# Moving three block loads from GpSimd's queue to SyncE's, and a new place for the quarters in the load order

## The chip, the cores and the metric

The kernel runs on one NeuronCore of a Trainium2 chip. The core has five engines with a queue of instructions each: TensorE (PE: matmuls, and transposes through a matmul), VectorE (DVE), ScalarE (ACT), GpSimd (POOL) and SyncE (SP, which here only issues DMAs). They wait for each other by semaphores. Sixteen DMA engines move data between HBM and SBUF; SP, ACT and POOL each feed them through a queue of their own. The metric is the device time of one execution in microseconds, the median of several runs; lower is better.

## The reference

```python
y = np.matmul(x, weight)                      # x: 16 x 512 x 768 fp32, weight: 768 x 768
y = y.reshape(batch, seq, n_heads, head_dim)  # 12 heads of 64
y1, y2 = y[..., :32], y[..., 32:]
out1 = y1 * cos1 - y2 * sin1                  # cos, sin: 512 x 64, one row per position
out2 = y2 * cos2 + y1 * sin2
out = np.concatenate([out1, out2], axis=-1)   # 16 x 512 x 768 fp32
```

A projection, and then a rotation of every head by its position (RoPE). 25.2 MB are read for x and 25.2 MB written.

## The kernel before

**Tiles and groups.** The 8192 rows of x are cut into 64 tiles of 128 rows. A tile is one batch and one residue of the position modulo 4, so that all rows of a tile's partition have the same cos and sin. Four tiles (four batches, one residue) make a group `g`, 0 to 15; a group has two pairs of tiles, `(g, 0)` and `(g, 1)`.

**How a tile gets to TensorE.** A matmul wants x transposed and in fp16. A plain tile is loaded whole in fp32 by SP (`load`, L211, 384 KB, one of ten buffers xs), cast to fp16 by ScalarE (`cast`, through the helper `copy`, L191, xs to xc), transposed by TensorE (`turn`, L257, and `turn_rows`, L272) and copied out of PSUM by ScalarE (L191, pt to xt). A block pair, one of the pairs in `BLOCKS`, takes another way: it is loaded as four quarters of 32 partitions each (`load_quarter`, L226), in runs of 192 elements, and transposed in blocks of 32 x 32 by VectorE (`turn_pair`, L300, to xp), so that TensorE and PSUM are spared. There are two kinds of block pair:

- "pool": GpSimd issues the quarters, and the DMA casts them to fp16 on the way into one of three buffers xh. No cast is needed. VectorE transposes xh.
- "sp": SP issues the quarters in fp32, 192 KB each, into one of three buffers xb; ScalarE casts the pair (`cast_pair`, xb to xd, 128 x 1536 elements), and VectorE transposes xd.

Before the change, the pairs `(g, 1)` of groups 4, 6, 8, 10 and 12 are "pool"; those of 5, 7, 9, 11, 13 and 15 are "sp". All other pairs are plain.

**The order of SP's loads.** A list `fetch` is written once, ahead of the main loop: plain tiles in order, and behind each a quarter of the next "sp" pair, as long as there is one, from the group before on. `pump` walks down this list when a cast has been written: it stops at a plain tile when ten are loaded and not yet cast (`NX`), and at the first quarter of a pair when three pairs are (`NB`). SP works strictly in the order of the list. The quarters of "pool" pairs aren't in it: `pool_loads` writes them for GpSimd's queue, up to 20 tiles ahead (`P_AHEAD`), between GpSimd's additions.

**The main loop** runs over the tiles from 4 on, in the order of the matmuls. For each it writes the matmuls of the tile (`walk` and `one`, L362, in halves of 64 rows), the turning of a plain tile three tiles ahead, the casts five tiles ahead (`casts`), the block transposes four tiles ahead (`bturns`) and the stores. The last half group has matmuls of 128 rows (L337).

**Behind the matmuls.** VectorE reads a bank of PSUM and writes the products with cos and with sin (`rope`, L443, into tq or the space of w_raw), GpSimd adds the two (L465, into ov), and the results are stored by ScalarE's queue (`store`, L497), from group 13 on by SP's. The last group has smaller pieces, some of which are added by VectorE or TensorE (L405, L412, L475).

Of the kernel before, what the change touches and what calls it, by code (L numbers as in the profile page):

```python
# [16 lines left out]
class Flow:  # L17
# [24 lines left out]
    def do(self, e, make, reads=(), writes=(), dma=None, tick=True, after=0):  # L42
        need = {}
        for k in reads:
            for s, v in self.wrote.get(k, {}).items():
                need[s] = max(need.get(s, 0), v)
        for k in writes:
            for d in (self.wrote, self.readby):
                for s, v in d.get(k, {}).items():
                    need[s] = max(need.get(s, 0), v)  # L50
        if e == "pe":
            need.pop("pe", None)
            if after:
                need["pe"] = after
        waits = self.settle(e, need)
        for s, v in waits[:-1]:
            self.eng[e].wait_ge(self.sem(s), v)  # L57
        i = make(self.eng[e])
        if waits:
            s, v = waits[-1]  # L60
            i.wait_op(self.sem(s), v, "sem-ge")
        name, step = (dma, 16) if dma else (e, 1)
        self.sem(name)
        self.order[name] = len(self.order) + sum(self.count.values())
        at = self.count[name] + step
        if tick or dma:
            i.then_inc(self.sems[name], step)
            self.count[name] = at
            self.known[name, at] = dict(self.seen[e])
        for k in reads:  # L70
            d = self.readby.setdefault(k, {})
            d[name] = max(d.get(name, 0), at)
        for k in writes:
            self.wrote[k] = {name: at}
            self.readby[k] = {}
        return i
# [32 lines left out]
def kernel(  # L109
# [11 lines left out]
    f = Flow(nc, tc)  # L121
# [18 lines left out]
    BLOCKS = {}  # L140
    for g in range(5, 14):
        BLOCKS[g, 1] = "pool" if g % 2 == 0 and g >= 4 else "sp"
    BLOCKS[LAST, 1] = "sp"
    BLOCKS[4, 1] = "pool"

    def sbuf(name, shape, dt):
        return nc.alloc_sbuf_tensor(name, shape, dt).ap()
# [50 lines left out]
    def pair_of(i):  # L198
        return i // QB, (i % QB) // 2

    def is_block(i):
        return pair_of(i) in BLOCKS
# [28 lines left out]
    def load_w(c, e="sp"):  # L231
        t, h = c
        do(e, lambda eng: eng.dma_start(out=w_raw[:, t, h], in_=wv[t, h]),  # L233
           writes=[f"wr{t}{h}"], dma=f"ov{t}_0" if h else f"xb{t}")

    def cast_w(c, e):
        t, h = c
# [271 lines left out]
    for k in order:  # L509
        if isinstance(k, int):  # L510
            load(k)
        else:
            load_w(CHUNKS[int(k[1])])
# [4 lines left out]


    fetch, quarters = [], []  # L520
    soon = [p for p in sorted(BLOCKS) if BLOCKS[p] == "sp"]
    for i in range(QB, NTILE):
        if soon and i >= max(2, soon[0][0] - 1) * QB:
            quarters += [(soon[0], q) for q in (0, 2, 1, 3)]
            soon.pop(0)
        if not is_block(i):
            fetch.append(i)
            for _ in range(2 if i == QB * (LAST - 1) else 1):
                if quarters:
                    fetch.append(quarters.pop(0))  # L530
        elif quarters and quarters[0][0] == pair_of(i):
            fetch.append(quarters.pop(0))
    fetched = [0]
# [120 lines left out]
    for g in range(LAST):  # L654
        for h in (0, 2):
            i = QB * (g + 1) + h
            q = (g, h * H, (h + 2) * H, "act")
# [4 lines left out]
            elif g < LAST - 2:  # L662
                i = QB * (LAST - 2) + 2 * (g - LAST + 4) + h // 2
            else:
                q = q[:3] + ("sp",)
# [22 lines left out]
    for i in range(QB, NTILE):  # L688
# [17 lines left out]
        for n, p in enumerate(pieces(g, s)) if i >= ROWS else ():  # L706
            a, z, _, bank = p
# [66 lines left out]
```

## Time and profile before

| | |
|---|---|
| median of 3 runs | 150.17 us (149.97 to 152.46) |
| the profiled execution | 149.84 us |
| its span, first to last instruction | 148.1 us |
| TensorE busy, matmuls | 140.8 us (95%) |
| VectorE busy | 126.8 us (86%) |
| GpSimd busy | 123.3 us (83%) |
| ScalarE busy | 75.9 us (51%) |
| HBM read and written | 27.79 MB and 25.17 MB, 358 GB/s over the span |
| clock granted to TensorE | full, in all slices |

How to read it: a group row names line, engine, operation, output and input, shape and count, and then the busy time in us, the mean time of one in ns, and the idle time of the engine before it. A row of the timeline has start and length in us, and in brackets the time that the engine was idle before, with the engine that ended it. A row of windows has the busy time of PE, PEld (weight loads), DVE, ACT and POOL, each with the number of instructions, and then the clock, the share of the 16 DMA engines and what they moved in GB/s. A row of transfers has the number of issues, the size of one as it is written to its destination, and the median time from issue to landing. The share of the DMA engines sums the recorded times of packets, which overlap, so it can pass 1. Busy time is an average over the whole run; which engine decides is read from the chain and from the waits.

### The profile page before, as it was taken

How to read it: one execution, taken by the hardware profiler on the slowest of the kernel's cores; microseconds unless marked ns; L12 is line 12 of the kernel's file. 1: busy time of each engine (PE TensorE's matmuls, PEld its weight loads, DVE VectorE, ACT ScalarE, POOL GpSimd, SP SyncE). 2: the span in 40 equal slices, each digit the busy share in tenths (PEclk: the TensorE clock that was granted, in tenths of full speed). 3: DMA queues.
4: the chain of work that ended last, by engine and by line, in shares of the span. 5: the costliest groups of instructions: out<-in, count | busy, mean ns of one | idle time of the engine just before them, and what ended most of it. 6: DMA issues, size and time to landing. Idle time of an engine off the chain costs nothing.

```text
span 148.1 us, 4361 instructions
## 1 busy us (share of the span) xinstructions
PE 140.8 (95%) x1918; PEld 112.8 (76%) x1918; DVE 126.8 (86%) x102; ACT 75.9 (51%) x90; POOL 123.3 (83%) x76
## 2 busy tenths in 40 slices
PE   6879999999999999999999999999999999999980
PEld 2335578888888888888888888888888888765860
DVE  0244999884999999899999998999989999999990
ACT  3444798787761933557261915375263919931010
POOL 1000399999999999999999999869899999899980
PEclk9999999999999999999999999999999999999999
DMA  4999999999999999999999999999999999998684
GB/s 125 344 394 400 401 401 400 303 351 319 332 351 343 319 336 290 328 408 296 326 362 394 375 310 360 347 400 328 371 380 360 411 412 415 414 402 320 238 309 172
DMA packets 28355, 51.27 MB, mean 346 GB/s; under 512 B 7216, under 2 KB 14128, under 8 KB 28336
## 3 DMA queue, kind: packets, MB, share of 16 engines
q1 hardware_dynamic: 15536, 28.05, 55.2%
q10 hardware_dynamic: 7360, 20.97, 36.0%
q0 software_dynamic: 5440, 1.97, 10.7%
q8 instruction: 15, 0.25, 0.7%
q14 instruction: 4, 0.03, 0.1%
HBM read 27.79 MB, written 25.17 MB: 358 GB/s over the span
## 4 chain that ended last, share of the span: by engine, by line
PE 78%; DVE 12%; DMA 5%; issue 2%; SPq 1%; DVEq 0%
PE py L362 68%; DVE tq L443 8%; PE py L337 5%; DMA w_raw<-in_weight_dram 5%; PE pt L272 4%; DVE w_raw L443 2%; SPq L211 1%; PE pt L257 1%; SPq L233 1%; DVE ov L412 1%; DVE py L405 0%; DVE xs L405 0%; DVE w_sb L191 0%; DVEq L57 0%; SPq L769 0%
## 5 line engine op out<-in xcount | busy, mean ns | idle before, releaser
L465 POOL TENSOR_TENSOR ov<-tq 128x512 f32<-128x512 f32 (+3 forms) x34 | 76.1, 2261 | 19.5 <-DVE tq L443 19.4
L362 PE MATMUL py<-w_sb,xt 64*128 64x512 f16 (+1 forms) x816 | 77.7, 323 | 0.0
L443 DVE TENSOR_TENSOR tq<-py,csn 128x1024 f32<-128x1024 f32 (+2 forms) x51 | 74.3, 1495 | 3.2 <-PE py L362 2.8
L362 PEld LDWEIGHTS py<-w_sb,xt 64*128 64x128 f16 x816 | 57.2, 94 | 10.3 <-DVE tq L443 0.4
L191 ACT COPY xt<-pt 128x768 f16<-128x768 f16 x40 | 32.0, 801 | 50.2 <-PE pt L272 49.0
L362 PE MATMUL py<-w_sb,xp 64*128 64x512 f16 (+1 forms) x480 | 47.5, 323 | 0.0
L191 ACT CAST xc<-xs 128x768 f16<-128x768 f32 x42 | 36.8, 909 | 7.2 <-DMA xs<-in_x_dram 7.1
L443 DVE TENSOR_TENSOR w_raw<-py,csn 128x1024 f32<-128x1024 f32 (+1 forms) x22 | 35.3, 1606 | 4.5 <-POOL w_raw L718 2.1
L362 PEld LDWEIGHTS py<-w_sb,xp 64*128 64x128 f16 x480 | 34.2, 94 | 5.5
L465 POOL TENSOR_TENSOR ov<-w_raw 128x1536 f32<-128x1536 f32 (+2 forms) x15 | 35.4, 2375 | 0.7 <-DVE w_raw L443 0.5
L337 PE MATMUL py<-w_sb,xt 128*128 128x256 f16 (+1 forms) x102 | 17.0, 317 | 1.5 <-DVE w_sb L191 1.3
L272 PEld LDWEIGHTS pt<-ident,xc 64*128 64x128 f16 x432 | 14.1, 95 | 1.3 <-issue 0.2
L337 PEld LDWEIGHTS py<-w_sb,xt 128*128 128x128 f16 x102 | 9.2, 98 | 7.5 <-DVE w_sb L191 2.8
L272 PE MATMUL pt<-ident,xc 64*128 64x64 f16 x432 | 14.1, 190 | 0.0
L226 POOL DMA_DIRECT2D xh<-in_x_dram x20 | 11.7, 590 | 0.0
L191 ACT CAST xd<-xb 128x1536 f16<-128x1536 f32 x6 | 9.8, 1641 | 0.0
L191 DVE CAST w_sb<-w_raw 128x768 f16<-128x768 f32 x6 | 3.4, 558 | 3.8 <-DMA w_raw<-in_weight_dram 3.8
L300 DVE STREAM_TRANSPOSE xp<-xh 128x768 f32<-128x768 f32 x5 | 6.2, 1236 | 0.0
L560 PE MATMUL py<-cold 128*128 128x512 f16 x12 | 4.8, 566 | 1.4 <-DVE cold L502 1.4
L300 DVE STREAM_TRANSPOSE xp<-xd 128x768 f32<-128x768 f32 x6 | 5.8, 970 | 0.0
L191 ACT COPY ov<-py 128x256 f32<-128x256 f32 x1 | 0.4, 373 | 10.0 <-PE py L475 10.0
L191 DVE COPY xt<-pt 128x768 f16<-128x768 f16 x2 | 1.1, 558 | 5.0 <-PE pt L257 5.0
(26 smaller groups left out, 23.0 us busy)
## 6 DMA issues: line engine op xcount, KB each, us to landing
out_dram<-ov ACTq DMA_DIRECT2D x26, 768.0 KB, 9.2
xs<-in_x_dram SPq DMA_DIRECT2D x42, 384.0 KB, 16.0
xb<-in_x_dram SPq DMA_DIRECT2D x24, 192.0 KB, 16.7
out_dram<-ov SPq DMA_DIRECT2D x4, 768.0 KB, 5.3
w_raw<-in_weight_dram SPq DMA_DIRECT2D x6, 384.0 KB, 7.1
xh<-in_x_dram POOLq DMA_DIRECT2D x20, 96.0 KB, 12.9
out_dram<-ov SPq DMA_DIRECT2D x1, 384.0 KB, 2.3
out_dram<-ov ACTq DMA_DIRECT2D x1, 384.0 KB, 2.4
```

The costliest lines, as they stand in the source:

```text
L191: eng.copy(out=o, in_=i_) if e == "act" else eng.tensor_copy(out=o, in_=i_)
L211: do(e, lambda eng: eng.dma_start(out=xs_b[k], in_=x[b].rearrange("(p r) h -> r p h", r=SB)[r]), writes=[f"xs{k}"], dma=f"xs{k}")
L226: do(e, lambda eng: eng.dma_start(out=dst[ts(q, R)], in_=src[r, q]), writes=[f"{name}q{q}"], dma=name)
L233: do(e, lambda eng: eng.dma_start(out=w_raw[:, t, h], in_=wv[t, h]), writes=[f"wr{t}{h}"], dma=f"ov{t}_0" if h else f"xb{t}")
L257: do("pe", lambda eng: eng.transpose(pt[:, t, h, :], src[:, t, h, :], ident), reads=[f"xc{c}", "ident"], writes=[f"pt{k}"], tick=(t, h) == ...
L272: do("pe", lambda eng: eng.transpose(pts[r][:, t, h, :], src[rows, t, h, :], ident[rows, rows]), reads=[f"xc{c}", "ident"], writes=[f"pt{r ...
L300: do("dve", lambda eng: eng.transpose(out=dst, in_=src), reads=rd, writes=[f"xp{z}"])
L337: do("pe", lambda eng: eng.matmul(ps, get(t, h), w_sb[:, t, h, a - s * H : z - s * H], start=start, stop=stop), reads=[key, f"w{t}{h}"], w ...
L362: do("pe", lambda eng: eng.matmul(py[:, a:z], get(t, h)[rows], w_sb[rows, t, h, a - s * H : z - s * H], start=start, stop=not opens and en ...
L443: do("dve", lambda eng: eng.tensor_tensor(out=tq.rearrange("p j (h d) -> p j h d", d=D), in0=ps.rearrange("p (h d) -> p h d", d=D) .unsque ...
L465: do(adder, lambda eng: eng.tensor_tensor(out=ov_b[o][:, ds(c0, w)].rearrange("p (h t d) -> p h t d", t=2, d=HD), in0=tq[:, 0].rearrange(" ...
L560: do("pe", lambda eng: eng.matmul(py[:, ts(b, 512)], cold[:, 0:P], cold, start=True, stop=warmed[0] < WARM - 6), reads=["cold"], writes=[f ...
```

## The change

The pairs `(8, 1)`, `(10, 1)` and `(12, 1)` become "sp" pairs. Together with `(9, 1)`, `(11, 1)` and `(13, 1)` they are `DIRECT`: their quarters no longer follow other tiles in `fetch`, but stand where their own pair's two plain tiles would stand, quarters 0 and 2 in the place of the first, 1 and 3 in the place of the second. So from tile 32 on the list reads: two plain tiles, four quarters, two plain tiles, four quarters. The quarters of pairs `(5, 1)`, `(7, 1)` and `(15, 1)` stay where they were. The weight loads use other semaphores, those of the output buffers in place of xb's.

```diff
     BLOCKS[4, 1] = "pool"
+    DIRECT = ((8, 1), (9, 1), (10, 1), (11, 1), (12, 1), (13, 1))
+    for p in DIRECT:
+        BLOCKS[p] = "sp"
...
         do(e, lambda eng: eng.dma_start(out=w_raw[:, t, h], in_=wv[t, h]),
-           writes=[f"wr{t}{h}"], dma=f"ov{t}_0" if h else f"xb{t}")
+           writes=[f"wr{t}{h}"], dma=f"ov{t}_{1536 * (1 - h)}")
...
     fetch, quarters = [], []
-    soon = [p for p in sorted(BLOCKS) if BLOCKS[p] == "sp"]
+    soon = [p for p in sorted(BLOCKS) if BLOCKS[p] == "sp" and p not in DIRECT]
     for i in range(QB, NTILE):
...
             for _ in range(2 if i == QB * (LAST - 1) else 1):
                 if quarters:
                     fetch.append(quarters.pop(0))
+        elif pair_of(i) in DIRECT:
+            fetch += [(pair_of(i), q) for q in ((0, 2), (1, 3))[i % 2]]
         elif quarters and quarters[0][0] == pair_of(i):
             fetch.append(quarters.pop(0))
```

## The prediction

> **What bounds the kernel now.** I read the chain of waits first, then the table of waits, then VectorE's timeline, and last the DMA engines, which the first three leave out. By line, the chain gives 68.3% of the span to L362, the 64-row matmuls; in order of time it is TensorE without a gap from 10.6 to 125.8 us, then VectorE. In the table of waits no matmul of L362 stands at all. VectorE, from its timeline between 107 and 126 us:
>
> ```profile
> 108.73 1.23 DVE L443 TENSOR_TENSOR w_raw<-py,csn 128x1024 f32<-128x1024 f32 x1 [0.54 <-PE py L362]
> 109.88 1.24 DVE L300 STREAM_TRANSPOSE xp<-xh 128x768 f32<-128x768 f32 x1
> ...
> 116.89 2.36 DVE L443 TENSOR_TENSOR tq<-py,csn 128x1024 f32<-128x1024 f32 x2 [0.27 <-PE py L362]
> 119.16 0.97 DVE L300 STREAM_TRANSPOSE xp<-xd 128x768 f32<-128x768 f32 x1
> ...
> 124.94 0.98 DVE L300 STREAM_TRANSPOSE xp<-xd 128x768 f32<-128x768 f32 x1
> 125.84 1.19 DVE L443 TENSOR_TENSOR tq<-py,csn 128x1024 f32<-128x1024 f32 x1
> ```
>
> The brackets matter. Until 116.89 VectorE still waits for TensorE (0.54, 0.27 us), so time that it saves earlier turns into a longer bracket. From 116.89 it has no bracket before its last instruction at 144.2: a pause of VectorE after that moves the end by as much.
>
> Now the page's rows of transfers, and windows of the span (last three columns: clock, DMA share, GB/s):
>
> ```profile
> DMA  4999999999999999999999999999999999998684
> xb<-in_x_dram SPq DMA_DIRECT2D x24, 192.0 KB, 16.7
> xh<-in_x_dram POOLq DMA_DIRECT2D x20, 96.0 KB, 12.9
> ```
> ```profile
> 48.00:60.00 12.00, 12.00 (x190) 10.35 (x188) 11.28 (x9) 6.73 (x8) 11.99 (x7) 1.00 1.18 313
> 100.00:116.00 16.00, 16.00 (x240) 13.78 (x237) 15.33 (x11) 7.55 (x10) 15.15 (x7) 1.00 1.05 364
> 102.00:104.00 2.00, 2.00 (x28) 1.71 (x25) 2.00 (x2) 0.00 (x0) 2.00 (x1) 1.00 1.06 252
> 105.00:109.00 4.00, 4.00 (x72) 3.47 (x69) 3.46 (x3) 2.20 (x3) 3.99 (x2) 1.00 1.04 403
> 120.00:128.00 8.00, 8.00 (x141) 6.50 (x138) 7.83 (x8) 6.14 (x7) 7.55 (x7) 1.00 1.03 413
> ```
>
> The DMA engines are full from 4 to 133 us. SyncE's timeline says the same: between 84 and 108 us each issue begins as the last one ends, and one takes up to 4 us, because its queue is full:
>
> ```profile
> 91.67 0.45 SPq L211 DMA_DIRECT2D xs<-in_x_dram  x1
> 92.17 6.74 SPq L226 DMA_DIRECT2D xb<-in_x_dram  x2
> 98.95 0.50 SPq L211 DMA_DIRECT2D xs<-in_x_dram  x1
> ```
>
> So there is a second bound just under TensorE. How far under is the landing of each load against the start of its cast (issue records and ScalarE's timeline). Pair (9,1) lands 7.7 us ahead of its cast, pair (11,1) 6.5, pair (15,1) 3.6 (119.69 against 123.27), tile 61 3.4 (125.47 against 128.90). GpSimd's own quarters are far ahead: pair (12,1) lands at 97.1 and VectorE takes it at 109.9.
>
> **Part by part.** *Off GpSimd:* 12 issues of 590 ns, 7.1 us. Nobody in the table of waits stands behind GpSimd but VectorE once, 2.1 us for L718 at 36 us, so this is worth 0. *VectorE:* three transposes read xd in place of xh; by the rows
>
> ```profile
> L300 DVE STREAM_TRANSPOSE xp<-xh 128x768 f32<-128x768 f32 x5 | 6.2, 1236 | 0.0
> L191 ACT CAST xd<-xb 128x1536 f16<-128x1536 f32 x6 | 9.8, 1641 | 0.0
> L300 DVE STREAM_TRANSPOSE xp<-xd 128x768 f32<-128x768 f32 x6 | 5.8, 970 | 0.0
> ```
>
> that is 3 x 0.266 = 0.8 us, all before 111 us, where the brackets of 0.54 and 0.27 us take it up: worth 0, at best 0.8. *ScalarE:* three more casts of 1.641 us, 4.9 us. In groups 9 and 11 the same cast fills a pause of 3.6 us in which ScalarE waits for TensorE, and no matmul waits behind it: 0. If that cover were gone, 1.6 us a pair would still lie ahead of VectorE's transpose, which comes 2.0 us after such a cast. *Semaphores of the weight loads:* other names, same instructions, no wait: 0.
>
> *SyncE's queue* is where the time is. Twelve quarters move into a queue that is already full, and the order changes: a group's two plain tiles, then its four quarters. Issue time itself (0.43 us each) hides behind the full queue. A further limit: xb has three buffers, so pair (10,1) may start once the cast of (7,1) is done (67.1 us), and its cast would come at 89.9, half way between those of (9,1) and (11,1): 22.8 us, more than the 16.7 us from issue to landing, so the wait alone does not decide.
>
> What the DMA engines pay, from the packet records. (a) 120 to 128 us has 1069 packets of 3072 B and nothing else: 8 x 16 / 1069 = 119.7 ns of one engine each. (b) 100 to 116 us has 1555 of those and 1300 of 768 B (SyncE's quarters): (256 - 186.1) / 1300 = 53.8 ns. (c) 48 to 60 us has 820, 903 and 1367 of GpSimd's, which read 768 B and write 384: (192 - 98.2 - 48.6) / 1367 = 33.1 ns. A quarter has 256 packets. Changing 12 quarters from (c) to (b): 3072 x 20.7 ns / 16 = 4.0 us more DMA time. The bounds: the recorded durations of single packets (mean 45.4 ns for SyncE's, 49.1 for GpSimd's) would make it 0.7 us less; the stretch at 102 to 104 us, when no store runs (244 quarter packets and 103 of 3072 B: 81 ns), makes it 9.2 us more. I take 4.0, since (a) to (c) share out whole microseconds of a full engine and packets overlap in the records (share 1.18 of one).
>
> The 252 GB/s of that stretch is a quarter's weakness: fp32 into 32 partitions, alone, is slow; beside stores it is not (403 GB/s at 105 to 109 us). [...]
>
> From DMA time to lateness: stores bring 512 packets per 8.15 us (one group), 61 of 130 engine-us, and they alternate with the loads packet by packet (97 to 98 us: 94 against 95), so they are served in full and the loads have 53%. 4.0 / 0.53 = 7.5 us later by the last pair, built up over groups 8 to 13. Against it: pair (15,1) has 3.6 us ahead of its cast and then nothing (cast ends 124.91, VectorE transposes at 124.94). 7.5 - 3.6 = 3.9 us of pause on VectorE behind 116.89, and the end moves by it. TensorE's other feeds are milder: tile 57 lands 4 us ahead of its cast, which lies 5 us ahead of its turning. Behind VectorE's transpose stand all the products of groups 13 to 15, GpSimd's adds and the last stores.
>
> The sum: 0 + 0 + 0 + 3.9. The profiled execution was 149.84 (span 148.1 and 1.7 around it), so about 153.8; the median shown is 0.33 above it: **154.2 us**, 2.7% slower. Two per cent, 3.0 us, is about what a measurement tells from no change.
>
> **Rivals.** *A, the quarters cost no more than before* (not slower): if the price per packet is that of the single records, 45.4 against 49.1, the DMA engines win 0.7 us, loads stay ahead in the order in which they are used, and the end is VectorE's as now: 150.0, at best 149.4 with the 0.8 us of the transposes. For it: in stretches with stores (97 to 101 us) the quarters' packets are recorded at 36 ns; two quarters in a row land in different partitions. Against: (b) measures whole stretches. It decides where the extra falls below 3.6 x 0.53 = 1.9 us, that is 10 ns a packet. [...] Chance 0.30.
>
> *B, late, but covered in part:* extra of 2 to 3.5 us gives 0.2 to 3 us, 150.4 to 153.1. Chance 0.10.
>
> *C, the forecast:* over 3 us late, 153.2 to 159; 0.53. Once TensorE stops, stores stop too and the loads catch up, so the 9.2 us bound doesn't multiply: 9.2 - 3.6 = 5.6 at full catching up, 9 with half of it.
>
> *D, the buffers of xb stall the queue as well:* pairs 10 to 13 each late by the 2 us that lie between a cast and VectorE's transpose, 160 or more; 0.04. Against it, the 22.8 us.
>
> *E, GpSimd's freed 7.1 us reach the end:* by over 3 us, 146.5; the chain shows no such path. 0.03.
>
> So faster 0.03 (E), within 2% 0.40 (A and B), slower 0.57 (C and D). The range, 149.4 to 159.0, leaves out D, E and the ends; the forecast's own part is 153.2 to 159.
>
> **What would show it.** Right: loads of groups 12 to 15 land after ScalarE would take them, ScalarE's casts wait for the DMA of xb or xs behind 105 us, VectorE has a bracket before its transpose of pair (15,1), more stretches near 250 GB/s between 75 and 120 us, GpSimd 7 us less busy without gain. Wrong: VectorE without a bracket from 117 us on, or pair (15,1) landing before 123 us (A); TensorE idle from 85 us on (D); a shorter chain on VectorE (E).

## The result

The changed kernel takes 154.55 us (median of 4 runs, 153.71 to 157.36) against 150.07 us for the kernel before (4 runs, 149.40 to 152.46). The ratio is 1.0295, with a 95% interval of 1.0221 to 1.0369: slower by 3%, where 2.7% was forecast. The ratios here and below leave out runs more than 1.5% above the fastest of their kernel; the kernel before has such runs too, 10 of the 41 beside the experiments and up to 154.85 us, none of them profiled, so what lengthens them stays open.

The first profile of the changed kernel is of its longest execution (157.36 us, span 155.6), in which TensorE ran at half clock (0.50) for 6.83 us; so the kernel was profiled a second time (the last experiment below: 152.42 us, span 150.6, full clock throughout). What both profiles show, the change did; what only the first shows is treated at the end.

VectorE's timeline of the changed kernel, first profile (start and length in us, and in brackets the idle time before and who ended it):

```profile
116.86 2.36 DVE L446 TENSOR_TENSOR tq<-py,csn 128x1024 f32<-128x1024 f32 x2 [0.54 <-PE py L365]
...
121.16 3.84 DVE L446 TENSOR_TENSOR w_raw<-py,csn 128x1024 f32<-128x1024 f32 x3
129.80 0.98 DVE L303 STREAM_TRANSPOSE xp<-xd 128x768 f32<-128x768 f32 x1 [4.80 <-ACT xd L194]
130.70 3.45 DVE L446 TENSOR_TENSOR tq<-py,csn 128x1024 f32<-128x1024 f32 x3
136.84 3.49 DVE L446 TENSOR_TENSOR tq<-py,csn 128x1024 f32<-128x1024 f32 x3 [2.69 <-PE py L365]
```

And of the second profile:

```profile
120.97 3.83 DVE L446 TENSOR_TENSOR w_raw<-py,csn 128x1024 f32<-128x1024 f32 x3
127.54 0.98 DVE L303 STREAM_TRANSPOSE xp<-xd 128x768 f32<-128x768 f32 x1 [2.74 <-ACT xd L194]
128.44 6.98 DVE L446 TENSOR_TENSOR tq<-py,csn 128x1024 f32<-128x1024 f32 x6
```

Up to 121 us VectorE keeps the times of the kernel before within 0.3 us; the 0.27 us that each of three transposes now saves has gone into its waits for TensorE (0.54 in place of 0.27 at 116.9). Then it stands before the transpose of pair (15,1), 4.80 us in the one and 2.74 in the other, for ScalarE's cast. In the second profile that is the whole loss: the span is 2.5 us longer than before. ScalarE's timeline of the second profile says what it waited for:

```profile
121.14 0.92 ACT L194 CAST xc<-xs 128x768 f16<-128x768 f32 x1 [3.87 <-DMA xs<-in_x_dram]
...
124.96 0.89 ACT L194 CAST xc<-xs 128x768 f16<-128x768 f32 x1 [2.20 <-DMA xs<-in_x_dram]
...
125.96 1.54 ACT L194 CAST xd<-xb 128x1536 f16<-128x1536 f32 x1
```

The casts of tiles 57 and 58 and of pair (15,1) each start as their load lands. TensorE stands still nearly as long as VectorE, 4.35 us in the first profile and 2.64 in the second, for ScalarE's copy of a turned tile (xt), which in ScalarE's order stands behind the same cast. The table of waits of the first profile has it:

```profile
PE pt L275 <- ACT xt L194: 4.4, 1, 4.4
```

How the loads lost their lead, from the issue records and ScalarE's casts (us from landing to the start of the cast; "late" is against the same landing in the kernel before):

| | pair 9 | pair 11 | pair 13 | pair 15 lands | late | last load lands |
|---|---|---|---|---|---|---|
| before | 7.7 | 6.5 | 7.7 | 119.69 | | 125.47 |
| changed, first profile | 4.6 | 1.8 | 0.0 | 128.20 | 8.5 | 133.06 |
| changed, second profile | 7.9 | 3.7 | 1.5 | 125.94 | 6.3 | 131.68 |

In the first and the third of the following stretches the DMA engines are as full as before and move less. Windows of the kernel before (last columns: clock, DMA share, GB/s):

```profile
60.00:64.00 4.00, 4.00 (x53) 3.44 (x50) 4.00 (x3) 1.11 (x2) 4.00 (x3) 1.00 1.07 360
64.00:68.00 4.00, 4.00 (x73) 3.46 (x69) 3.72 (x4) 3.27 (x4) 3.99 (x4) 1.00 1.07 378
92.00:96.00 4.00, 4.00 (x52) 3.39 (x49) 3.56 (x3) 1.71 (x3) 3.62 (x2) 1.00 1.11 345
```

and of the changed one, second profile:

```profile
60.00:64.00 4.00, 4.00 (x53) 3.42 (x51) 4.00 (x3) 0.91 (x2) 2.82 (x1) 1.00 1.06 274
64.00:68.00 4.00, 4.00 (x73) 3.44 (x70) 3.73 (x4) 3.46 (x4) 3.66 (x2) 1.00 1.04 406
92.00:96.00 4.00, 4.00 (x53) 3.41 (x51) 3.75 (x3) 1.64 (x3) 3.44 (x2) 1.00 1.10 304
```

The GB/s count a load by what it writes to SBUF, so the kernel before, with its fp16 quarters, read more from HBM than they say (pages of both: 27.79 MB read from HBM in either, but packets of 51.27 MB before and 52.45 MB in the changed kernel). POOL's column shows that GpSimd is less busy, 4.00 to 2.82 us at 60 to 64 us, which nobody used.

### The profile page after: what moved, and what is told of

It reads as the page before. It is cut to its first block, busy times and chain, and to the rows that moved or that the text cites. A ratio compares the mean times of both kernels' runs of the same rounds, so it can differ in the third digit from the quotient of the medians.

```text
span 155.6 us, 4364 instructions
## 1 busy us (share of the span) xinstructions
PE 144.1 (93%) x1918; PEld 115.2 (74%) x1918; DVE 126.1 (81%) x102; ACT 80.7 (52%) x93; POOL 116.7 (75%) x64
## 2 busy tenths in 40 slices
DMA packets 28355, 52.45 MB, mean 337 GB/s; under 512 B 4144, under 2 KB 14128, under 8 KB 28336
## 3 DMA queue, kind: packets, MB, share of 16 engines
HBM read 27.79 MB, written 25.17 MB: 340 GB/s over the span
## 4 chain that ended last, share of the span: by engine, by line
PE 41%; SPq 24%; DMA 14%; DVE 12%; issue 3%; POOL 2%; ACT 2%; DVEq 0%; ACTq 0%; POOLq 0%
PE py L365 33%; SPq L214 13%; SPq L229 10%; DMA xb<-in_x_dram 9%; DVE tq L446 7%; PE py L340 4%; DMA w_raw<-in_weight_dram 4%; PE pt L275 3%; DVE w_raw L446 2%; POOL ov L468 2%; ACT xd L194 1%; PE pt L260 1%; DVE xp L303 1%; SPq L236 1%; DVE ov L415 1%
## 5 line engine op out<-in xcount | busy, mean ns | idle before, releaser
L365 PE MATMUL py<-w_sb,xt 64*128 64x512 f16 (+1 forms) x816 | 80.5, 329 | 0.1
L365 PEld LDWEIGHTS py<-w_sb,xt 64*128 64x128 f16 x816 | 58.5, 96 | 11.5 <-issue 1.4
L365 PE MATMUL py<-w_sb,xp 64*128 64x512 f16 (+1 forms) x480 | 48.0, 324 | 0.0
L365 PEld LDWEIGHTS py<-w_sb,xp 64*128 64x128 f16 x480 | 35.2, 94 | 4.9
L275 PEld LDWEIGHTS pt<-ident,xc 64*128 64x128 f16 x432 | 14.6, 96 | 5.8 <-ACT xt L194 4.6
L275 PE MATMUL pt<-ident,xc 64*128 64x64 f16 x432 | 14.8, 193 | 4.4 <-ACT xt L194 4.4
L194 ACT CAST xd<-xb 128x1536 f16<-128x1536 f32 x9 | 14.6, 1624 | 3.0 <-DMA xb<-in_x_dram 2.9
L303 DVE STREAM_TRANSPOSE xp<-xd 128x768 f32<-128x768 f32 x9 | 8.7, 969 | 4.8 <-ACT xd L194 4.8
L229 POOL DMA_DIRECT2D xh<-in_x_dram x8 | 4.8, 600 | 0.0
L565 PEld LDWEIGHTS py<-cold 128*128 128x128 f16 x12 | 1.6, 141 | 3.6 <-issue 2.2
```

Of the source, the lines that this page charges most:

```text
L194: eng.copy(out=o, in_=i_) if e == "act" else eng.tensor_copy(out=o, in_=i_)
L229: do(e, lambda eng: eng.dma_start(out=dst[ts(q, R)], in_=src[r, q]), writes=[f"{name}q{q}"], dma=name)
L275: do("pe", lambda eng: eng.transpose(pts[r][:, t, h, :], src[rows, t, h, :], ident[rows, rows]), reads=[f"xc{c}", "ident"], writes=[f"pt{r ...
L303: do("dve", lambda eng: eng.transpose(out=dst, in_=src), reads=rd, writes=[f"xp{z}"])
L365: do("pe", lambda eng: eng.matmul(py[:, a:z], get(t, h)[rows], w_sb[rows, t, h, a - s * H : z - s * H], start=start, stop=not opens and en ...
L565: do("pe", lambda eng: eng.matmul(py[:, ts(b, 512)], cold[:, 0:P], cold, start=True, stop=warmed[0] < WARM - 6), reads=["cold"], writes=[f ...
```

## The experiments

Four theories were set against each other. P: SyncE's fp32 quarters cost the DMA engines more time a packet (one run of 768 bytes) than GpSimd's fp16 ones. O: the place in the load order makes the loads late. Q: the loss of GpSimd's own queue does, whatever the bytes. S: three xb buffers are too few. Later P was sharpened to R.

### Only the order (e1_order)

```diff
-    DIRECT = ((8, 1), (9, 1), (10, 1), (11, 1), (12, 1), (13, 1))
+    DIRECT = ((9, 1), (11, 1), (13, 1))
```

> Only the order: pairs (9,1), (11,1), (13,1) stand in their own place in the load order; the pairs of groups 8, 10 and 12 stay GpSimd's fp16 quarters. Theory P (price: SyncE's fp32 quarters cost the DMA engines some 20 ns a packet more than GpSimd's): no packet changes its price, so 149.5 to 151 us, pair (15,1) lands 3 to 4 us ahead of its cast, no pause of VectorE there. Theory O (the place in the order makes them late): 153 to 155. Theory Q (the loss of GpSimd's separate queue, whatever the bytes) and theory S (three xb buffers for all pairs): as P here.

149.71 us (149.49 to 150.36), ratio to the kernel before 0.9991 (0.9971 to 1.0011). Pair (15,1) lands at 120.68, 2.75 us ahead of its cast, a little less than the 3 to 4 expected; VectorE has no pause. O falls.

### Only the kind (e2_kind)

```diff
     for p in DIRECT:
         BLOCKS[p] = "sp"
+    DIRECT = ()
```

> Only the kind: the pairs of groups 8, 10 and 12 are SyncE's fp32 quarters, all quarters interleaved with plain tiles as before. P: the DMA time is that of the change, so 152.5 to 156 us with a pause of VectorE before its transpose of pair (15,1). O: 149.5 to 151. Q and S: 152.5 to 156 as P.

158.19 us median, from 153.56 to 158.66 in four runs. In the profile the lead shrinks as in the changed kernel (pair 9 3.9, pair 11 0.7, pair 12 0.0) and VectorE stands before pair (15,1):

```profile
131.91 0.98 DVE L304 STREAM_TRANSPOSE xp<-xd 128x768 f32<-128x768 f32 x1 [5.63 <-ACT xd L195]
```

So the kind alone makes the loads late, by 10.6 us in this execution (pair (15,1) lands at 130.31). Whether the old order is worse than the new one would need more runs to claim.

### Four xb buffers (e7_nb4)

```diff
-    NX, NB, NBH, NC, NCP, NXT, NXP, NOV = 10, 3, 3, 5, 2, 8, 4, 4
+    NX, NB, NBH, NC, NCP, NXT, NXP, NOV = 10, 4, 2, 5, 2, 8, 4, 4
```

> The changed kernel with four xb buffers in place of three (and two xh in place of three). P, O and Q: 153.5 to 156 us, as the change. S: the queue of SyncE no longer waits for a buffer and the loads come earlier, 150 to 152.

155.15 us (153.73 to 157.25), ratio 1.0341 (1.0200 to 1.0482). Pair (15,1) lands at 125.40, 5.7 us late, and VectorE pauses 2.14 us. S falls as the cause, since the loss stays; whether a buffer more wins a little, the interval can't say.

### GpSimd issues the same fp32 quarters (e4_pool_fp32)

```diff
+    for g in (8, 10, 12):
+        BLOCKS[g, 1] = "gp"
...
-        e = BLOCKS[gh]
+        kind = BLOCKS[gh]
+        e = "sp" if kind == "sp" else "pool"
+        bufs, n = {"pool": ("xh", NBH), "sp": ("xb", NB), "gp": ("xg", 2)}[kind]
```

> The kernel before, but GpSimd issues the quarters of groups 8, 10 and 12 in fp32, without the cast in the transfer, into buffers of their own; ScalarE casts them. Queue, order and lead are those of before, the bytes written are those of the change. P (it is the bytes written into 32 partitions): pair (15,1) late by some 4 us, 152 to 155 us. Q, O and S: 149.5 to 151.

Inconclusive. The four runs lie at 149.59, 152.62, 154.28 and 154.57; the profiled one is the first, in which pair (15,1) lands at 121.89, 2.2 us late but still 1.16 us ahead of its cast. The experiment was not as clean as meant: in the packet records GpSimd's fp32 quarters are not 768-byte packets but 384 of 4608 and 192 of 3072 bytes (12 quarters), so besides queue and bytes the packets changed too. It excludes neither P nor Q, and of the three longer runs there is no profile.

### Transfers alone (m1_loads)

A kernel with nothing but transfers, in stretches that begin when the one before has landed.

> The disputed price by itself: transfers alone, nothing computed (matmul, rotation and all results are left out). Six stretches, each begun when the one before has landed: 16 plain tiles; 32 fp32 quarters by SyncE in the order 0, 2, 1, 3; 32 fp16 quarters by GpSimd; the fp32 quarters again beside 8 stores; the fp16 quarters beside 8 stores; the fp32 quarters in the order 0, 1, 2, 3. P: alone, the fp32 quarters read 200 to 270 GB/s (32 quarters of 196.6 KB in 23 to 31 us, 45 to 61 ns of one engine per packet), GpSimd's 330 GB/s or more (33 to 37 ns); beside stores the gap is half or less. Theory A (same price): both within 10% of each other alone.

Windows within the first three stretches, plain tiles, SyncE's fp32 quarters and GpSimd's fp16 quarters, and within the last one, fp32 in the order 0, 1, 2, 3 (columns: GpSimd's busy time, clock, DMA share, GB/s written):

```profile
4.00:18.00 14.00, 0.00 (x0) 1.00 1.02 400
24.00:46.00 22.00, 0.00 (x0) 1.00 1.11 232
50.00:70.00 20.00, 17.20 (x31) 1.00 1.39 157
165.00:190.00 25.00, 0.00 (x0) 1.00 1.12 219
```

SyncE's quarters land every 0.85 us: 16 x 850 / 256 = 53.1 ns a packet, where the prediction had shared out 53.8. GpSimd's land every 0.62 us on average, hardly slower than GpSimd issues them (0.57 us): 38.8 ns at most, where it had 33.1. They read 314 GB/s, twice what is written, where 330 or more was expected, so this stretch does not show how fast they can be; m2_beside below has them with a backlog. That the two kinds differ alone, by far more than 10%, speaks against equal prices. The order of the quarters counts for 6% (232 against 219 GB/s). The two stretches beside stores gave nothing, because the quarters in them began only behind the stores.

### One pair and two pairs (d1_one, d2_two)

```diff
-    DIRECT = ((8, 1), (9, 1), (10, 1), (11, 1), (12, 1), (13, 1))
+    DIRECT = ((9, 1), (11, 1), (12, 1), (13, 1))                # d1_one
+    DIRECT = ((9, 1), (10, 1), (11, 1), (12, 1), (13, 1))       # d2_two
```

> The change for the pair of group 12 alone; 8 and 10 stay GpSimd's. P: a third of the extra DMA time, 1.3 us, some 2.5 us of lateness, less than the 3.6 us that pair (15,1) has in hand: 149.7 to 151 us, that pair landing 0.5 to 2 us ahead of its cast. A threshold-free cause (each moved pair costs a third of the whole): 151.5.

> The change for the pairs of groups 10 and 12; 8 stays GpSimd's. P: 2.7 us of DMA time, some 5 us of lateness against 3.6 us in hand: 151 to 152.5 us with a pause of VectorE of 1 to 2 us before its transpose of pair (15,1). A cause without a threshold: 153.

One pair: 149.75 us (149.52 to 150.05), ratio 0.998 (0.9943 to 1.0018); pair (15,1) lands 2.79 us ahead of its cast. Two pairs: 153.04 us, from 149.71 to 156.24; in the profile (of the run at 156.24) that pair lands at 127.19, and VectorE pauses 3.90 us. One pair costs nothing, as a threshold has it, and two cost more than the 151 to 152.5 us expected. In the profiles the lateness isn't shared out by thirds: 0.75 us for one pair, 7.5 for two (8.5 and 6.3 for three), where 2.5 and 5 were expected. But there is one profile of each, for two pairs of the longest of its runs, so whether the lateness makes a step is not shown. The scatter of the two-pair kernel, from no loss to 6 us, would fit a kernel on the threshold.

### The last pair by GpSimd (e6_last_pool)

```diff
-    BLOCKS[LAST, 1] = "sp"
+    BLOCKS[LAST, 1] = "pool"
...
-        if i == QB * (LAST - 2) + 2:
-            cast_pair((LAST, 1))
-            xb_used[0] += 1
```

> The changed kernel, but pair (15,1) is issued by GpSimd in fp16, from tile 42 on, and VectorE transposes it from xh (no cast by ScalarE, 0.27 us more on VectorE). P: that pair lands long before its use and SyncE's queue is four quarters shorter, so the pause of VectorE before it goes; what is late next are tiles 57 to 61 by at most 1 us: 149.8 to 151.5 us. A cause elsewhere (ScalarE's extra casts, GpSimd, the buffers): 153 to 155 stays.

A miss: 156.76 us (153.09 to 158.87). The pause left pair (15,1), as expected, but came two groups earlier. VectorE's timeline:

```profile
122.15 0.98 DVE L303 STREAM_TRANSPOSE xp<-xd 128x768 f32<-128x768 f32 x1 [2.87 <-ACT xd L194]
123.05 1.19 DVE L446 TENSOR_TENSOR tq<-py,csn 128x1024 f32<-128x1024 f32 x1
128.34 3.84 DVE L446 TENSOR_TENSOR w_raw<-py,csn 128x1024 f32<-128x1024 f32 x3 [4.11 <-PE py L365]
132.10 1.26 DVE L303 STREAM_TRANSPOSE xp<-xh 128x768 f32<-128x768 f32 x1
```

GpSimd issues this pair at 103.8 us, just when SyncE's queue holds pair (13,1), and the two were under way together: the pair that VectorE takes at 132 us lands at 121.62, and the one that it would take at 119 lands at 120.54, where the changed kernel had it at 115.82 and 112.60. The last load comes 4.3 to 5.7 us earlier than in the changed kernel's profiles (127.34). How much of that is the cheaper quarters, and how much the stores that TensorE's earlier standstill held back, is not separated. Here the queue of a load decided its turn, and that the turn went to the wrong pair hides what P would have gained.

### The quarters over all partitions (e8_spread)

The low rates of the windows above come where few or no stores run. Sorting the half microseconds of 60 to 122 us by whether 15 or more packets of a store begin in them (packet records, GpSimd's packets counted as the 768 bytes that they read): with stores, the kernel before and the changed one move 389 and 391 GB/s. Without, the kernel before has 12.0 us, 7.5 of them with GpSimd's quarters beside SyncE's at 339 GB/s and 4.5 with SyncE's alone at 303; the changed kernel has 17.0 us at 270 (second profile 15.5 at 275). Theory R: an fp32 quarter into 32 partitions is slow when nothing runs beside it. Theory B is its rival: packets of 768 bytes are dear, wherever they land. To test it, the same bytes were spread over all partitions:

```diff
+        to, fr = dst[ts(q, R)], src[r, q]
+        if gh in DIRECT:
+            to = dst[:, 2 * q : 2 * q + 2]
+            fr = x[b + q // 2].rearrange("(p r) (q k) -> r p q k", r=SB, q=NQ)[r][:, q % 2 :: 2]
-        do(e, lambda eng: eng.dma_start(out=dst[ts(q, R)], in_=src[r, q]),
+        do(e, lambda eng: eng.dma_start(out=to, in_=fr),
```

> The changed kernel, but each quarter of groups 8 to 13 lands on all 128 partitions, two runs of 768 bytes in each, in place of 32 partitions with eight runs: the same bytes read once, the same queue, order, size and number of packets (the rows then stand in the wrong place, so the outputs of these pairs are not the reference's). Theory R (the price of SyncE's quarters is paid where no store runs beside them, because 32 partitions take only some 230 GB/s): no stretch under 300 GB/s between 60 and 122 us, pair (15,1) lands before 121 us, 149.5 to 150.7 us. Theory B (768-byte packets from HBM, or their number, are what is dear): as the change, 153.5 to 156 us.

149.98 us (149.18 to 150.29), ratio to the kernel before 1.0007 (0.9982 to 1.0033): the whole loss is gone, with queue, order, packets, casts and GpSimd's relief as in the changed kernel. Pair (15,1) lands at 114.86, 8.2 us ahead of its cast, the last load at 120.60, and every load of groups 9 to 13 is 8 to 12 us ahead. VectorE in this kernel, and two of the windows in which the changed kernel had 274 and 304 GB/s:

```profile
120.91 3.82 DVE L450 TENSOR_TENSOR w_raw<-py,csn 128x1024 f32<-128x1024 f32 x3
124.69 0.98 DVE L307 STREAM_TRANSPOSE xp<-xd 128x768 f32<-128x768 f32 x1
```

```profile
60.00:64.00 4.00, 4.00 (x54) 3.47 (x51) 4.00 (x3) 0.85 (x2) 2.75 (x1) 1.00 1.05 394
92.00:96.00 4.00, 4.00 (x54) 3.47 (x51) 3.82 (x3) 1.56 (x2) 3.35 (x1) 1.00 1.06 410
```

No bracket. The store-free time runs at 348 GB/s. B falls as the cause, since the packets are as many and as short, and Q falls with this kernel as well: GpSimd's queue is gone here too, and nothing is lost. The spread also changes which runs a quarter reads from HBM; that this is what helps is unlikely, since GpSimd's fp16 quarters read the same runs as the fp32 ones at some 360 GB/s (m2_beside). R's bound of no stretch under 300 was too strict: there are a few (250 GB/s at 108 to 112 us), without harm. It is no version to use, since the rows stand in the wrong partitions, and with GpSimd relieved and the loads early it is still not faster than the kernel before.

### Beside each other (m2_beside)

> Transfers alone again (no matmul, no rotation, no results). Stretches: 16 plain tiles; 32 fp32 runs-of-768 transfers over 128 partitions each; 32 fp32 quarters issued by GpSimd; 16 fp32 quarters of SyncE beside 4 stores; 16 fp16 quarters of GpSimd beside 4 stores; 32 fp32 quarters of SyncE, with 16 fp16 quarters of GpSimd beside the second half. R: the spread transfers at 330 GB/s or more (SyncE's quarters alone were 231); beside stores reads and writes together at 360 to 400 GB/s; the last stretch's second half at 300 GB/s or more of reads. B: the spread transfers at 230 to 250 GB/s, as the quarters.

Windows within the stretches: spread transfers; fp32 quarters by GpSimd; SyncE's fp32 quarters beside stores, and the same behind the stores; GpSimd's fp16 quarters alone; SyncE's fp32 with GpSimd's fp16 quarters:

```profile
24.00:40.00 16.00, 0.00 (x0) 1.00 1.06 323
48.00:70.00 22.00, 14.19 (x25) 1.00 1.04 230
76.00:84.00 8.00, 0.00 (x0) 1.00 1.05 400
86.00:94.00 8.00, 0.00 (x0) 1.00 1.12 236
109.00:115.00 6.00, 0.00 (x0) 1.00 1.53 180
124.00:136.00 12.00, 1.98 (x4) 1.00 1.31 235
```

The spread transfers reach 323, a little under the 330 expected; plain tiles had 400 in m1_loads, so the short runs, or the order in which they are read, may cost something too. An fp32 quarter goes at 230 to 236 GB/s, whoever issues it, though GpSimd's packets there have 4608 and 3072 bytes and SyncE's 768: once more not the length of the packets, and not the queue. The same quarter beside stores makes 400 together, and its packets are recorded at 36 ns, where they are at 57 alone. GpSimd's fp16 quarters write 180 and so read some 360 GB/s, twice what is written: 2807 packets in these 6 us, 34.2 ns each. Both kinds together read 314 (packet records, 124 to 136 us). Beside stores the fp16 quarters were a miss: 338 GB/s together (98 to 108 us), where 360 to 400 was expected. So a store beside it hides the weakness of the fp32 quarter, and GpSimd's fp16 stream beside it hides a part; the change took the second away.

### The changed kernel once more (a2_again)

> The changed kernel once more, for a second profile: the first one's execution (157.4 us) was the longest of four and ran TensorE at half clock for some 7 us after a standstill. Theory R: the lateness is there before TensorE first stands still, so pair (15,1) lands 6 us or more after 119.7 us again and VectorE pauses 2.5 to 5 us before its transpose; 153.5 to 155 us if TensorE's standstill is short, with the half clock shorter as well. A disturbance of that one execution: no pause, or under 1 us.

152.42 us; the one run of the kernel before beside it took 151.64, so the two times say nothing together. In the profile pair (15,1) lands 6.3 us late, VectorE pauses 2.74 us, TensorE stands still for 2.64 us (125.61 to 128.26) and keeps full clock. The time is 1.1 us under the 153.5 to 155 us expected; the late pair and the two waits are the same as in the first profile.

## Why the prediction was right

*The parts worth nothing.* Right. GpSimd is 6.6 us less busy (123.3 to 116.7) without gain; e8_spread, with the same relief, is at 1.0007. The three transposes' 0.8 us went into VectorE's waits for TensorE: those from 70 to 118 us sum to 1.9 us before and 2.8 after. ScalarE's three casts hold nobody up in e8_spread, which has them too, and the weight loads' other semaphores cost nothing in e1_order, which has those (0.9991).

*The wait for xb's buffers.* Right that it doesn't decide (e7_nb4, with a fourth buffer, is at 1.0341), and rival D with it.

*The price of a packet.* Right, 53.8 and 33.1 ns against 53.1 (m1_loads) and 34.2 (m2_beside) measured alone. But it is no fixed price of a quarter: beside stores the packets are recorded at 36 ns, and spread over all partitions the loss is gone. The 4.0 us of DMA time were somewhat too much. At a pace of about 390 GB/s, the changed kernel's 17.0 us at 270 lose 17.0 x (1 - 270/390) = 5.2 us, the kernel before loses 7.5 x (1 - 339/390) + 4.5 x (1 - 303/390) = 2.0; the difference is 3.2 us, and by the second profile 15.5 x (1 - 275/390) = 4.6, 2.6 more than before. (The limit of 15 packets is a choice: with 6 or 21 the first difference is 2.4 or 3.3.) The prediction weighed the weakness of the quarter alone, but put it beside the price rather than as its cause. Alone the fp32 quarters ran at 230 to 236 GB/s (m1_loads, m2_beside), and at 219 in the order 0, 1, 2, 3, and spreading the same packets over all partitions took the loss away. GpSimd's fp16 quarters land in 32 partitions too and wrote 180 GB/s, under the rate of the fp32 ones, so the same weakness need not show in them: an estimate from these two rates. What in the hardware makes the weakness is not seen in any trace here.

*From DMA time to lateness.* Forecast 7.5 us, measured 8.5 and 6.3. But the step between is not confirmed: 3.2 and 2.6 us over 0.53 would be 6.0 and 4.9 us. A term that was too large and a factor that left something out made up for each other, and so far the nearness of 7.5 is luck; where the rest of the lateness comes from is not shown. *From lateness to the end.* Forecast a pause of 3.9 us before the transpose of pair (15,1), measured 4.80 and 2.74, in that place, for that cast. Rival A, that the quarters cost no more than before, falls: it is not the queue that costs (fp32 quarters go at 230 and 236 GB/s by either), but the width (323 when the same bytes are spread over all partitions).

*Where it was off.* The forecast called TensorE's feeds milder than VectorE's, but TensorE stood still nearly as long, because ScalarE takes its casts and copies in one order (the result above). It had no term for what that standstill costs beyond itself (below): the 157.36 us are the 149.84 of the kernel before, a pause of 4.80 and the wait of 2.69 that followed on half clock. The other three runs have no profile. One of them, 154.28 us, was granted 0.999 of the clock over its span, so its 4.2 us over the kernel before came without half clock, near the 3.9 forecast. How the median of 154.55 divides into pause and half clock has not been separated, and that it lies within 0.4 us of 154.2 is in part luck.

## What to carry to other kernels

A queue of loads that is always full can be a bound that the chain of waits does not name, as here, where the 3.6 us that pair (15,1) had in hand stood in no wait; read how far each load lands ahead of its use, and watch whether that lead falls from group to group. Here a transfer into 32 partitions in fp32 was cheap beside stores (400 GB/s together) and dear alone (230), so before giving a load another form ask what runs beside it. Taking 6.6 us of work off GpSimd was worth nothing, because nobody waited for it.

## What the runs showed of the hardware that was not expected

TensorE's standstill was paid twice here. The granted clock in windows of the changed kernel's first profile, around the standstill from 126.17 to 130.52 us:

```profile
126.00:128.00 2.00, 0.17 (x3) 0.00 (x0) 0.00 (x0) 0.72 (x1) 0.42 (x1) 1.00 1.04 417
130.00:132.00 2.00, 1.48 (x20) 1.04 (x22) 2.00 (x3) 2.00 (x4) 0.00 (x0) 0.50 1.03 418
136.00:138.00 2.00, 2.00 (x37) 1.51 (x31) 1.17 (x2) 0.99 (x3) 0.00 (x0) 1.00 0.87 346
```

In the clock records, half clock begins at 129.16 and lasts 6.83 us, and VectorE, which had caught up, then waits 2.69 us for TensorE (its last bracket above). In e7_nb4 a standstill of 2.04 us was followed by 3.41 us at half clock, in e2_kind one of 5.07 by 3.41, in d2_two one of 3.81 by 6.83, in e6_last_pool one of 4.69 by 6.83; in a2_again one of 2.64 us by none. So the length alone does not decide. In each of these traces the changes of the clock lie whole multiples of 3.41 us apart (in the first profile full clock for 122.88 us, half for 6.83 and full for 20.48, which is 36, 2 and 6 times 3.413), so a grid of windows of that length can be laid over it. Then TensorE's idle time within one window sorts them: half clock follows windows with 2.04 (e7_nb4), 2.20 (d2_two), 2.98 (the changed kernel), 3.26 (e6_last_pool) and 3.34 us (e2_kind), and none follows the two into which the 2.64 us of a2_again fall, 1.63 and 1.01, or the window with the first 1.74 us of e2_kind's standstill. Where the next window has no idle time, half clock lasts one window, 3.41 us (e7_nb4, e2_kind); where the standstill reaches 1.37 to 1.61 us into it, two, 6.83 us. A limit somewhere between 1.74 and 2.04 us of idle time in a window would fit all six profiles; that is an estimate from them, and no record shows the limit itself.

GpSimd's fp32 runs of 768 bytes stand in the records as packets of 4608 and 3072 bytes (e4_pool_fp32: 384 and 192 for 12 quarters), where with a cast, or from SyncE, each run is a packet of its own (the kernel before: 5120 packets of 384 bytes for 20 of GpSimd's quarters, 6144 of 768 for 24 of SyncE's).
